# Stores moved from SyncE's DMA queue to ScalarE's in a row softmax with a relative-position bias

## The chip, the core and the metric

The kernel runs on one core of a Trainium2 chip. The metric is the device time of one execution in microseconds (us), the median of several runs. The profile is of one execution of its own.

## What is computed

```python
B, H, S = (2, 8, 2112); max_rel = 16
rel = pos[:, None] - pos[None, :]
bias = rel_bias[:, np.clip(rel, -max_rel, max_rel) + max_rel]
logits = logits + bias[None, :, :, :]
logits = logits - logits.max(axis=-1, keepdims=True)
exp = np.exp(logits)
return exp / exp.sum(axis=-1, keepdims=True)
```

The input `logits` and the output have 2 x 8 x 2112 x 2112 float32 elements, 285.5 MB each. Every element is read once and written once; a row of 2112 elements is one softmax.

## The kernel before

**Tiling.** The 128 partitions hold two heads at a time: 64 partitions for each, and every partition owns 33 consecutive rows of its head (64 x 33 = 2112). An outer loop `k` runs over the 4 pairs of heads. Inside it, 12 chunks `m` (`NT = 12`) run over the 2 batches and over six groups of 6, 5, 6, 5, 6 and 5 of the 33 rows. A chunk is one load and one store of 128 x (6 or 5 rows x 2112) float32, 6336 or 5280 KB; in all there are 48 chunks. Four buffers `X0` to `X3` (`NBUF = 4`) are used in turn, and a chunk is loaded, computed in place and stored from the same buffer.

**Work on a chunk.** VectorE (DVE) adds the bias strip `F` and takes the row's maximum in one instruction for each row (`add`, L173). ScalarE (ACT) does the exp of each row with its sum (`exps`, L181). DVE takes the reciprocals (`scale`, L189) and scales the first three rows (`DV = 3`, L193); ACT scales the other two or three (`scale_rest`, L198). For each pair of heads DVE first builds the strip `F` (`strip`).

**Order.** Every engine has its own hand-written loop, and semaphores tie them: `ld[b]` and `st[b]` count finished loads and stores of buffer b, `added` and `expd` rows, `scaled` and `scaledA` the rows scaled by DVE and ACT. `take(engine, sem, n)` (L82) makes an engine wait for n and take them off again; its waits show as L83.

**DMA queues.** All 48 loads and all stores are issued by SyncE (SP), so they stand in one queue (q1) in program order. ACT's queue (q10) has only the small transfer of the bias table at the start. SP starts with four loads (`load`, L88). Then `turn` does for each n: wait for the scales of chunk n and issue its store (`store`, L96); wait until store n-1 has landed; issue load n+3 into the buffer that has come free. The last chunk's store is issued in two parts, the three rows of DVE and then the others.

Of the kernel before, what the change touches and what calls it, by code (L numbers as in the profile page):

```python
# [11 lines left out]
ENG = mybir.EngineType  # L12
# [3 lines left out]
def kernel(  # L16
# [6 lines left out]
    nc = tc.nc  # L23
    P = 128
    B, H, S, S2 = logits.shape
# [4 lines left out]
    K = H // 2  # L30
# [3 lines left out]
    NBUF = 4  # L34
# [4 lines left out]
    CH = [(b, sum(SIZES[:i]), r) for b in range(B) for i, r in enumerate(SIZES)]  # L39
    NT = len(CH)  # L40
# [3 lines left out]
    X = [io.tile([P, R * S], FP32, tag=f"X{b}", name=f"X{b}") for b in range(NBUF)]  # L44
# [14 lines left out]
    def rows(t, k, m, s0, n):  # L59

        b, j, r = CH[m]
        return bass.AP(
            tensor=t.tensor,
            offset=t.offset + (b * H * S + j + s0) * S + k * (2 * S * S),
            ap=[[W * S, P], [1, n * S]],
        )

    with tc.tile_critical(no_gpsimd_drain=True):  # L68
        ld = [nc.alloc_semaphore(f"ld{b}") for b in range(NBUF)]
        st = [nc.alloc_semaphore(f"st{b}") for b in range(NBUF)]  # L70
        added = nc.alloc_semaphore("added")
        expd = nc.alloc_semaphore("expd")
        scaled = nc.alloc_semaphore("scaled")
        scaledA = nc.alloc_semaphore("scaledA")
# [7 lines left out]
        def take(eng, sem, n):  # L82
            eng.wait_ge(sem, n).then_inc(sem, -n)  # L83


        def load(k, m):
            b, r = m % NBUF, CH[m][2]
            nc.sync.dma_start(out=X[b][:, 0 : r * S], in_=rows(logits, k, m, 0, r)).then_inc(ld[b], 16)  # L88

        def store(k, m, s0=0, n=None):  # L90
            b, n = m % NBUF, n or CH[m][2]
            if s0 < DV:
                take(nc.sync, scaled, DV)
            if s0 + n > DV:
                take(nc.sync, scaledA, s0 + n - DV)
            nc.sync.dma_start(  # L96
                out=rows(out, k, m, s0, n), in_=X[b][:, s0 * S : (s0 + n) * S]
            ).then_inc(st[b], 16)

        for m in range(NBUF):  # L100
            load(0, m)
# [6 lines left out]
            out=bass.AP(tensor=F.tensor, offset=F.offset, ap=[[Q * step, P // Q], [1, H * W]]),  # L108
            in_=bass.AP(tensor=rel_bias.tensor, offset=rel_bias.offset, ap=[[0, P // Q], [1, H * W]]),
# [57 lines left out]
        DV = 3  # L167
# [10 lines left out]
        def exps(m):  # L178
            for i in range(CH[m][2]):
                take(nc.scalar, added, 1)  # L180
                nc.scalar.activation(  # L181
                    out=row(m, i), in_=row(m, i), func=ACTF.Exp, scale=-1.0, bias=col(nmax, m, i),
                    accum_out=col(tot, m, i),
                ).then_inc(expd, 1)

        def scale(m):
            r = CH[m][2]
            take(v, expd, r)
            v.reciprocal(out=col(rec, m, 0, r), in_=col(tot, m, 0, r)).then_inc(inv, 1)  # L189
            v.wait_ge(inv, 1).then_inc(inv, -1)  # L190
            v.sem_inc(invA, 1)
            for i in range(DV):
                v.tensor_scalar_mul(out=row(m, i), in0=row(m, i), scalar1=col(rec, m, i)).then_inc(scaled, 1)  # L193

        def scale_rest(m):
            take(nc.scalar, invA, 1)
            for i in range(DV, CH[m][2]):
                nc.scalar.activation(  # L198
                    out=row(m, i), in_=row(m, i), func=ACTF.Copy, scale=col(rec, m, i),
                ).then_inc(scaledA, 1)  # L200

        with nc.Fori(0, K, 1, engines=[ENG.DVE]) as k:
            strip(k)
            for m in range(NT):
                add(m)
                scale(m)
        with nc.Fori(0, K, 1, engines=[ENG.Activation]):  # L207
            for m in range(NT):
                exps(m)
                scale_rest(m)  # L210

        def turn(k, first, stop):
            for n in range(first, stop):
                store(k + n // NT, n % NT)
                take(nc.sync, st[(n - 1) % NBUF], 16)
                load(k + (n + 3) // NT, (n + 3) % NT)

        store(0, 0)  # L220
        with nc.Fori(0, K - 1, 1, engines=[ENG.SP]) as k:
            turn(k, 1, NT + 1)
        turn(K - 1, 1, NT - 3)
        for m in range(NT - 3, NT - 1):
            store(K - 1, m)
        r = CH[NT - 1][2]
        store(K - 1, NT - 1, 0, DV)
        store(K - 1, NT - 1, DV, r - DV)
        for b in range(NBUF):
            take(nc.sync, st[b], 32 if b == (NT - 1) % NBUF else 16)  # L230


# [28 lines left out]
```

## Time and profile before

| | |
|---|---|
| time, median of 3 runs | 1329.12 us (1329.1 to 1329.44) |
| profiled execution, its time | 1329.3 us |
| its span | 1327.5 us |
| DVE busy / ACT busy | 819.7 us (62%) / 808.8 us (61%) |
| DMA, mean rate over the span | 430 GB/s |
| bytes read from and written to HBM | 285.48 MB and 285.47 MB |

The span is the part of the execution that the profile covers; 1.8 us lie around it. Where a row of the profile names an engine with a q (SPq, ACTq), it is that engine's instruction queue, which issues DMAs and waits on semaphores. A line of DMA issues gives the time from the issue to the landing, including the time in which the transfer stands behind others.

### The profile page before, as it was taken

To read this page: it belongs to the slowest core of one execution; us is meant where nothing else is said; L and a number is where in the kernel's file an instruction comes from. 1 tells how busy PE (TensorE), PEld (TensorE's weight loads), DVE (VectorE), ACT (ScalarE), POOL (GpSimd) and SP (SyncE) were. 2 spreads that over 40 slices of the span, in tenths; PEclk is the share of its full clock that TensorE was granted. 3 is DMA by queue.
4 is the path that set the end of the run, shared out by engine and by line. 5 is a ranking of instruction groups with operands and counts; after the bars stand their busy time and mean duration, and the time that the engine had idled before them with its cause. 6 is when DMAs were issued, how large, how long until landed. Compare 5 with 4: busy or idle time off the path is not lost. (4 is left out here: it accounts for less than half of the span.)

```text
span 1327.5 us, 2383 instructions
## 1 busy us (share of the span) xinstructions
DVE 819.7 (62%) x756; ACT 808.8 (61%) x652; POOL 0.6 (0%) x6
## 2 busy tenths in 40 slices
DVE  6875665558655566556866466664686547665572
ACT  3885575655756557555676566764667646675472
POOL 0000000000000000000000000000000000000000
DMA  9999999999999999999999999999999999999998
GB/s 407 427 424 425 430 433 429 432 431 433 434 430 438 423 439 431 432 432 433 438 436 429 433 430 435 433 430 441 427 439 428 435 431 437 434 436 427 436 427 376
DMA packets 13981, 571.00 MB, mean 430 GB/s; under 512 B 1556, under 2 KB 1560, under 8 KB 1560
## 3 DMA queue, kind: packets, MB, share of 16 engines
q1 hardware_dynamic: 13968, 570.96, 99.8%
q14 instruction: 5, 0.04, 0.0%
q10 hardware_dynamic: 8, 0.00, 0.0%
HBM read 285.48 MB, written 285.47 MB: 430 GB/s over the span
## 5 line engine op out<-in xcount | busy, mean ns | idle before, releaser
L173 DVE CUSTOM_DVE_ANT_0 X<-X,F 128x2112 f32<-128x2112 f32 x264 | 605.5, 2354 | 346.8 <-DVEq L83 346.8
L181 ACT ACTIVATE X<-X,nmax 128x2112 f32<-128x2112 f32 x264 | 542.2, 2054 | 411.5 <-ACTq L83 385.7
L198 ACT ACTIVATE X<-X,rec 128x2112 f32<-128x2112 f32 x120 | 238.7, 2046 | 29.0 <-ACTq L83 29.0
L193 DVE TENSOR_SCALAR X<-X,rec 128x2112 f32<-128x2112 f32 x144 | 181.4, 1316 | 11.6 <-DVEq L190 11.6
L189 DVE RECIPROCAL rec<-tot 128x6 f32<-128x6 f32 (+1 forms) x48 | 9.1, 190 | 116.1 <-DVEq L83 116.1
L181 ACT ACTIVATION_READ_ACCUMULATOR X<-X,nmax 128x1 f32 x264 | 49.3, 187 | 0.0
L181 ACT ACT_TABLE_LOAD x4 | 5.1, 1283 | 55.8 <-ACTq L83 55.8
L173 DVE DVE_READ_ACCUMULATOR2_ANT nmax<- 128x1 f32 x264 | 21.7, 82 | 0.0
L157 DVE TENSOR_TENSOR F<-F,rest 128x2112 f32<-128x2112 f32 x4 | 9.4, 2358 | 0.6
L149 DVE TENSOR_TENSOR F<-Z,rbK 128x2112 f32<-128x2112 f32 x4 | 9.4, 2358 | 0.6
L134 DVE LOAD_MASK_SELECT F<-F x1 | 0.0, 14 | 7.1 <-DMA F<-in_rel_bias_dram 7.1
L155 DVE SCALAR_TENSOR_TENSOR rest<-Z,rbK,rest 128x64 f32<-128x64 f32 x4 | 1.1, 284 | 0.6 <-DVEq L83 0.2
L151 DVE TENSOR_SCALAR rest<-Z,rbK 128x64 f32<-128x64 f32 x4 | 1.1, 275 | 0.0
L105 DVE MEMSET F<- 128x264 f32 x1 | 0.3, 278 | 1.1 <-SPq L68 1.1
L145 DVE COPY rbK<-rbP 128x33 f32 x4 | 0.7, 178 | 0.3 <-DVEq L83 0.3
L153 DVE COPY F<-rbK 128x16 f32<-128x16 f32 x4 | 0.7, 168 | 0.0
L152 DVE COPY F<-rbK 128x16 f32<-128x16 f32 x4 | 0.7, 166 | 0.0
L132 DVE TENSOR_SCALAR Z<-F 128x64 f32<-128x64 f32 x3 | 0.5, 223 | 0.1
L140 DVE COPY rbP<-F 64x132 f32<-64x132 f32 x2 | 0.4, 224 | 0.2
L134 DVE STREAM_SHUFFLE F<-F 128x264 f32<-128x264 f32 x1 | 0.4, 443 | 0.0
L112 POOL IOTA F<- 64x64 f32 x2 | 0.4, 179 | 0.7 <-PEq L256 0.6
L245 POOL MEMSET const-bfloat16-1.0<- 128x1 bf16 x1 | 0.1, 103 | 0.0
(3 smaller groups left out, 0.3 us busy)
## 6 DMA issues: line engine op xcount, KB each, us to landing
X<-in_logits_dram SPq DMA_DIRECT2D x24, 6336.0 KB, 39.7
out_dram<-X SPq DMA_DIRECT2D x24, 6336.0 KB, 46.9
X<-in_logits_dram SPq DMA_DIRECT2D x24, 5280.0 KB, 42.2
out_dram<-X SPq DMA_DIRECT2D x23, 5280.0 KB, 48.6
out_dram<-X SPq DMA_DIRECT2D x1, 3168.0 KB, 16.5
out_dram<-X SPq DMA_DIRECT2D x1, 2112.0 KB, 21.1
F<-in_rel_bias_dram ACTq DMA_DIRECT2D x1, 4.1 KB
```

Source lines behind the costliest of these rows:

```text
L145: then(v.tensor_copy(out=rbK[:, :], in_=rbP[:, bass.ds(k, 1), :]))
L149: then(v.tensor_tensor(out=blocks, in0=view(eq, 0, [[1, NB], [0, W]]), in1=view(rbK, W - 1, [[0, NB], [-1, W]]), op=ALU.mult))
L151: then(v.tensor_scalar(out=rest, in0=lt, scalar1=low, scalar2=None, op0=ALU.mult))
L152: then(v.tensor_copy(out=F[:, 0:MR], in_=low.to_broadcast([P, MR])))
L153: then(v.tensor_copy(out=F[:, FW - MR : FW], in_=high.to_broadcast([P, MR])))
L155: then(v.scalar_tensor_tensor(out=rest, in0=gt, scalar=high, in1=rest, op0=ALU.mult, op1=ALU.add))
L157: then(v.tensor_tensor(out=blocks, in0=blocks, in1=view(rest, 0, [[1, NB], [0, W]]), op=ALU.add))
L173: v.tensor_tensor_reduce(out=row(m, i), in0=row(m, i), in1=F[:, W - 1 - j - i : W - 1 - j - i + S], scale=-1.0, scalar=BIG, op0=ALU.add, o ...
L181: nc.scalar.activation(out=row(m, i), in_=row(m, i), func=ACTF.Exp, scale=-1.0, bias=col(nmax, m, i), accum_out=col(tot, m, i),).then_inc( ...
L189: v.reciprocal(out=col(rec, m, 0, r), in_=col(tot, m, 0, r)).then_inc(inv, 1)
L193: v.tensor_scalar_mul(out=row(m, i), in0=row(m, i), scalar1=col(rec, m, i)).then_inc(scaled, 1)
L198: nc.scalar.activation(out=row(m, i), in_=row(m, i), func=ACTF.Copy, scale=col(rec, m, i),).then_inc(scaledA, 1)
```

## The change

ACT issues each chunk's store itself, directly after its own scales of that chunk: it waits for the three rows of DVE and for its own, and starts the DMA on its own queue. SP keeps the loads alone: it waits until store n has landed and issues load n+4 into the same buffer. The last store is no longer split.

```diff
-        def store(k, m, s0=0, n=None):
-            b, n = m % NBUF, n or CH[m][2]
-            if s0 < DV:
-                take(nc.sync, scaled, DV)
-            if s0 + n > DV:
-                take(nc.sync, scaledA, s0 + n - DV)
-            nc.sync.dma_start(
-                out=rows(out, k, m, s0, n), in_=X[b][:, s0 * S : (s0 + n) * S]
-            ).then_inc(st[b], 16)
+        def store(k, m):
+            b, r = m % NBUF, CH[m][2]
+            take(nc.scalar, scaled, DV)
+            nc.scalar.wait_ge(scaledA, r - DV).then_inc(scaledA, -(r - DV))
+            nc.scalar.dma_start(out=rows(out, k, m, 0, r), in_=X[b][:, 0 : r * S]).then_inc(st[b], 16)
...
-        with nc.Fori(0, K, 1, engines=[ENG.Activation]):
+        with nc.Fori(0, K, 1, engines=[ENG.Activation]) as k:
             for m in range(NT):
                 exps(m)
                 scale_rest(m)
-
-
+                store(k, m)
 
         def turn(k, first, stop):
             for n in range(first, stop):
-                store(k + n // NT, n % NT)
-                take(nc.sync, st[(n - 1) % NBUF], 16)
-                load(k + (n + 3) // NT, (n + 3) % NT)
-
-        store(0, 0)
+                take(nc.sync, st[n % NBUF], 16)
+                load(k + (n + NBUF) // NT, (n + NBUF) % NT)
+
         with nc.Fori(0, K - 1, 1, engines=[ENG.SP]) as k:
-            turn(k, 1, NT + 1)
-        turn(K - 1, 1, NT - 3)
-        for m in range(NT - 3, NT - 1):
-            store(K - 1, m)
-        r = CH[NT - 1][2]
-        store(K - 1, NT - 1, 0, DV)
-        store(K - 1, NT - 1, DV, r - DV)
-        for b in range(NBUF):
-            take(nc.sync, st[b], 32 if b == (NT - 1) % NBUF else 16)
+            turn(k, 0, NT)
+        turn(K - 1, 0, NT - NBUF)
+        for m in range(NT - NBUF, NT):
+            take(nc.sync, st[m % NBUF], 16)
```

## The prediction

> **What bounds the kernel now.** I read the page first: its parts for the engines, the slices, the DMA queues and the DMA issues.
>
> ```profile
> span 1327.5 us, 2383 instructions
> DVE 819.7 (62%) x756; ACT 808.8 (61%) x652; POOL 0.6 (0%) x6
> ...
> DMA  9999999999999999999999999999999999999998
> GB/s 407 427 424 425 430 433 429 432 431 433 434 430 438 423 439 431 432 432 433 438 436 429 433 430 435 433 430 441 427 439 428 435 431 437 434 436 427 436 427 376
> DMA packets 13981, 571.00 MB, mean 430 GB/s; under 512 B 1556, under 2 KB 1560, under 8 KB 1560
> ...
> q1 hardware_dynamic: 13968, 570.96, 99.8%
> ...
> q10 hardware_dynamic: 8, 0.00, 0.0%
> ...
> X<-in_logits_dram SPq DMA_DIRECT2D x24, 6336.0 KB, 39.7
> out_dram<-X SPq DMA_DIRECT2D x24, 6336.0 KB, 46.9
> X<-in_logits_dram SPq DMA_DIRECT2D x24, 5280.0 KB, 42.2
> out_dram<-X SPq DMA_DIRECT2D x23, 5280.0 KB, 48.6
> out_dram<-X SPq DMA_DIRECT2D x1, 3168.0 KB, 16.5
> out_dram<-X SPq DMA_DIRECT2D x1, 2112.0 KB, 21.1
> ```
>
> No compute engine is busy for more than 62%, while packets of queue q1 fill 99.8% of what 16 DMA engines have in the span. The 40 slices are flat; only the first (407) and the last (376) lie well below 430 GB/s. So the kernel lasts as long as its 571 MB take. The windows and the wait lists say whether any stage is different.
>
> ```profile
> 200.00:1200.00 1000.00, 617.61 (x565) 612.19 (x493) 0.00 (x0) 1.00 1.00 433
> 1286.70:1305.30 18.60, 15.41 (x14) 14.74 (x12) 0.00 (x0) 1.00 1.00 433
> 1305.30:1327.50 22.20, 0.00 (x0) 0.00 (x0) 0.00 (x0) 1.00 0.80 346
> 310.90:325.90 15.00, 9.43 (x12) 5.22 (x4) 0.00 (x0) 1.00 1.01 433
> 325.90:340.90 15.00, 13.74 (x12) 12.54 (x12) 0.00 (x0) 1.00 1.00 431
> 340.90:353.70 12.80, 3.99 (x5) 7.04 (x5) 0.00 (x0) 1.00 1.01 429
> 353.70:366.20 12.50, 11.47 (x10) 9.51 (x9) 0.00 (x0) 1.00 1.00 431
> 366.20:381.10 14.90, 3.96 (x4) 5.24 (x4) 0.00 (x0) 1.00 1.01 435
> 381.10:396.10 15.00, 13.76 (x12) 11.84 (x11) 0.00 (x0) 1.00 1.01 436
> ```
>
> ```profile
> ACT X L181 <- ACTq L83: 385.7, 44, 12.5
> ```
>
> ```profile
> SPq L83 <- SPq L83: 1276.6, 141, 36.3
> ```
>
> The last two columns of a window are the DMA share and GB/s. In the middle of the run the DMA share is 1.00 and the rate 433 GB/s. The six short windows are cut where one transfer follows another: the first of each pair is mostly a load, the second mostly a store, and neither direction is slower (433, 429, 435 against 431, 431, 436). The waits say the same from the other side: SP waits 1276.6 of 1327.5 us, and ACT stands 385.7 us in front of its exps because data has not come.
>
> The timeline shows one round of the ring (the engine's waits stand in brackets).
>
> ```profile
> 310.88 0.35 SPq L88 DMA_DIRECT2D X<-in_logits_dram  x1
> ...
> 312.69 3.77 DVE L193 TENSOR_SCALAR X<-X,rec 128x2112 f32<-128x2112 f32 x3 [0.24 <-DVEq L190]
> 312.72 4.00 ACT L198 ACTIVATE X<-X,rec 128x2112 f32<-128x2112 f32 x2 [0.60 <-ACTq L83]
> ...
> 316.87 0.34 SPq L96 DMA_DIRECT2D out_dram<-X  x1
> ...
> 325.88 2.36 DVE L173 CUSTOM_DVE_ANT_0 X<-X,F 128x2112 f32<-128x2112 f32 x1 [3.52 <-DVEq L83]
> ...
> 340.88 0.35 SPq L88 DMA_DIRECT2D X<-in_logits_dram  x1
> ...
> 342.56 3.78 DVE L193 TENSOR_SCALAR X<-X,rec 128x2112 f32<-128x2112 f32 x3 [0.24 <-DVEq L190]
> 342.59 5.95 ACT L198 ACTIVATE X<-X,rec 128x2112 f32<-128x2112 f32 x3 [0.60 <-ACTq L83]
> ...
> 348.68 0.34 SPq L96 DMA_DIRECT2D out_dram<-X  x1
> 353.68 2.36 DVE L173 CUSTOM_DVE_ANT_0 X<-X,F 128x2112 f32<-128x2112 f32 x1 [7.34 <-DVEq L83]
> ...
> 366.19 0.35 SPq L88 DMA_DIRECT2D X<-in_logits_dram  x1
> ...
> 372.31 0.34 SPq L96 DMA_DIRECT2D out_dram<-X  x1
> ```
>
> A transfer of 6336 KB is 6.49 MB, 15.0 us at 433 GB/s, and one of 5280 KB is 12.5 us. Loads are issued at 310.88, 340.88 and 366.19: 30.0 and 25.3 us apart, a load and a store each. The median landing times (39.7 to 48.6 us) are some three transfers: everything stands in one line. A chunk holds its buffer outside that line from the first add to its store: 325.88 to 348.68 is 22.8 us for six rows, 353.68 to 372.31 is 18.6 us for five. Per pair of chunks that is 41.4 of 55.3 us, so on average 0.75 of the four buffers compute and 3.25 wait for or are in a transfer.
>
> **Part 1: two rings in place of one.** The sizes and the number of bytes stay; 48 loads stay on q1, 48 stores go to ACT's queue. Two queues bring no second set of engines: q1 already fills all 16. An engine is idle only when both of its rings are empty, which asks for all four buffers to be in compute at once; with 0.75 there on average that does not occur. So the sum changes only if a packet costs something else when its neighbour is of the other queue and direction. How finely the rings alternate is seen at the start.
>
> ```profile
> 0.97 1.88 SPq L88 DMA_DIRECT2D X<-in_logits_dram  x4
> ...
> 1.39 1.10 ACTq L107 DMA_DIRECT2D F<-in_rel_bias_dram  x1
> ...
> 9.08 0.01 DVE L134 LOAD_MASK_SELECT F<-F  x1 [7.10 <-DMA F<-in_rel_bias_dram]
> ...
> 18.60 2.36 DVE L173 CUSTOM_DVE_ANT_0 X<-X,F 128x2112 f32<-128x2112 f32 x1 [2.15 <-DVEq L83]
> ```
>
> The bias transfer of ACT's queue was issued at about 1.4 us, behind four loads of 23.8 MB, and had landed by 9.08 us, before the first load was used at 18.60. So rings do alternate, and within one transfer. The Trainium skill, page "DMA: Bandwidth & Descriptors", section "Queues, rings and completion order", says that an engine drains a whole packet, typically some 9 to 17 descriptors, from one ring before it goes to the next. By that rule the two rings would alternate about as coarsely as transfers follow each other now, and nothing about directions would change at all. The trace speaks for the finer alternation: a switch every 8 rows would have let the bias through only with the first load. I go by the trace.
>
> The page counts 13981 packets, of which 1556 are under 512 B (16 small ones for each of 97 transfers, and four more). That is 128 large packets to a transfer, 8 on each engine. Today an engine changes direction some 96 times; alternating packet by packet it would do so up to 768 times, 670 more. What a change costs, from both sides:
> - Nothing: the load and store windows above average 432.6 GB/s (weighted by length) and the long window, with the 74 transfers in it, has 433.
> - At most what the reading can hide: one unit in 433 GB/s is 2.3 us in 1000 us, over 74 changes 31 ns, and 670 of those are 21 us.
> - Below nothing: the best window, 436 GB/s, kept through the 1268 us from the first add (18.60) to the last load's landing (1286.7), would save 1268 x 3/436 = 8.7 us.
>
> I take nothing, since that is the row nearest to the case: the rate with changes in it equals the rate between them.
>
> **Part 2: the issue on ACT.** Each chunk puts two waits and one DMA issue behind ACT's scales, and behind these stand the next chunk's exps. An issue costs between 0.34 us (SP's rows) and 1.10 us (ACT's own first one): 48 of them 16 to 53 us on ACT. The 385.7 us of waiting in front of the exps cover that: after the scale that ends at 316.72 the next add comes only at 325.88. The wait for DVE's three scales is short or nil: DVE ends at 316.46 against ACT's 316.72 in five-row chunks, at 346.34 against 348.54 in six-row ones. In the first chunks there is no such cover:
>
> ```profile
> 41.38 16.61 SPq L96 DMA_DIRECT2D out_dram<-X  x2
> 41.48 2.06 ACT L181 ACTIVATE X<-X,nmax 128x2112 f32<-128x2112 f32 x1 [0.20 <-ACTq L83]
> ```
>
> The second chunk's exps would start up to 1.1 us later, and so its store. The four loads need 23.8 MB / 433 GB/s = 55 us, and the first store is there from about 41 us, so the rings are full: nothing on the path.
>
> **Part 3: SP.** SP loses 49 issues; load n+4 waits only for store n, no longer also for the issue of store n+1. That was never the later of the two: the store issued at 316.87 stands before the wait that ends at 340.88. Nothing.
>
> **Part 4: the end.** The last store is no longer split in 3 and 2 rows, so its first part leaves with the second. In the window from 1305.3, where it is issued, 346 GB/s x 22.2 us = 7.7 MB still move, of which the last store is 5.4 MB: 2.3 MB or 5.3 us of older stores stand before it. That covers the lost split, and up to 5.3 us of a later last load. Nothing.
>
> The sum is zero: the profiled execution took 1329.3 us, 1.8 over its span, and the median of the runs is 1329.12. Forecast **1329.0 us**.
>
> **Rivals.**
> *Alternating directions costs* (0.28). For it: no row shows loads and stores alternating packet by packet. Against it: both directions and the mixture run at the same rate. It begins to count at 4 ns for each of the 670 changes (2.7 us) and reaches 21 us at 31 ns. At the middle, 16 ns, it gives 1329 + 11 = 1340 us.
>
> *Alternating helps* (0.13): one ring's end of a transfer lies under the other's packets, and the rate rises to the best window's. 1329 - 8.7 = 1320 us. Against it: a DMA share of 1.00 leaves no gap to fill. The same page of the skill, section "Specifications", gives a ceiling of 435 GB/s; by it the gain would be at most about 6 us, an estimate. The windows at 436 are short enough for that to be rounding.
>
> *The end opens* (0.04): the last load, sharing with a store, lands more than 5.3 us later against the remaining stores, and the engines run dry for the rest. With 12 us later it gives 1329 + 7 = 1336 us.
>
> *The change does not do what it says* (0.03): stores from ACT are served in line with the loads as before, 1329 us. The bias transfer on q10 speaks against it.
>
> **How the numbers follow.** The forecast has 0.52. With the last rival, which gives the same time, "same" (within 0.2%, 2.7 us, about what a measurement here can tell) has 0.55, slower 0.28 + 0.04 = 0.32, faster 0.13. The range runs from 1324 (half of the helping case) to 1345 (16 of the 21 us); outside it lie about 0.07 below and 0.08 above.
>
> **What would show it right or wrong.** Right: q1 and q10 with about 285 MB each, 433 GB/s in the window 200 to 1200 us, loads that land in about 30 us (a 27.5 us pair side by side, plus the completion) in place of 40, stores in 55 to 60 (a buffer's round is four chunks of 27.65 us, less 20.7 of compute and the load's 30). Wrong: a middle window at 430 or less with a DMA share of 1.00 (packets got dearer), at 435 or more (cheaper), a share under 0.99 (both rings empty), or a last window with an earlier fall.

## The result and the profile after

The changed kernel takes 1340.05 us (median of 4 runs, 1337.98 to 1341.81) against 1329.28 us: 1.0079 of the time before, 95% interval 1.0064 to 1.0094. The forecast, no change, failed. The profiled execution took 1341.47 us, one of the slower of the four, with a span 12.1 us longer than before.

From the page of the changed kernel: span, engines, slices, queues, DMA issues (lines left out are marked).

```profile
span 1339.6 us, 2437 instructions
...
DVE 819.6 (61%) x756; ACT 808.4 (60%) x652; POOL 0.6 (0%) x6
...
DMA  9999999999999999999999999999999999999997
GB/s 404 405 422 433 436 432 431 437 431 427 441 430 430 430 436 424 438 430 424 439 432 427 430 428 433 425 431 434 427 427 426 433 427 428 431 425 428 437 433 308
...
q1 hardware_dynamic: 6912, 285.48, 50.0%
q10 hardware_dynamic: 6920, 285.48, 49.3%
...
X<-in_logits_dram SPq DMA_DIRECT2D x24, 6336.0 KB, 37.9
out_dram<-X ACTq DMA_DIRECT2D x24, 6336.0 KB, 49.4
X<-in_logits_dram SPq DMA_DIRECT2D x24, 5280.0 KB, 37.9
out_dram<-X ACTq DMA_DIRECT2D x24, 5280.0 KB, 53.8
```

The engines do the same work, the bytes are split evenly over two queues, and DMA is still the bound. The slices show two losses: many in the second half lie a little lower, and the last one has 308 GB/s where it had 376.

Two windows of the kernel before, then four of the changed one (last two columns: DMA share, GB/s):

```profile
20.00:100.00 80.00, 64.70 (x60) 67.90 (x55) 0.00 (x0) 1.00 1.01 429
1310.00:1320.00 10.00, 0.00 (x0) 0.00 (x0) 0.00 (x0) 1.00 0.94 406
```

```profile
20.00:100.00 80.00, 64.94 (x60) 67.56 (x55) 0.00 (x0) 1.00 1.00 417
200.00:1200.00 1000.00, 618.12 (x566) 610.88 (x494) 0.00 (x0) 1.00 1.00 430
1310.00:1320.00 10.00, 7.35 (x9) 9.00 (x10) 0.00 (x0) 1.00 0.69 299
1320.00:1330.00 10.00, 1.39 (x2) 1.65 (x1) 0.00 (x0) 1.00 0.84 360
```

In the middle the share is 1.00, as before, but the rate is 430 and not 433 GB/s: the engines are never idle, their packets take longer. The queues' part of the DMA view for the window 200 to 1200 us shows whose packets. First the kernel before, then the changed one (packets, MB, share of the 16 engines' time):

```profile
q1 hardware_dynamic: 10471, 433.13, 100.3%
```

```profile
q1 hardware_dynamic: 5200, 214.92, 50.4%
q10 hardware_dynamic: 5220, 215.33, 49.8%
```

Share divided by MB gives the price of a byte: per cent of the 16 engines' time in 1000 us for each MB. Before it is 100.3 / 433.13 = 0.2316. Afterwards stores (q10) pay 49.8 / 215.33 = 0.2313 and loads (q1) 50.4 / 214.92 = 0.2345, 1.3% more than before. Over 215 MB that is 0.63% of 1000 us, 6 us. The packet records show that not every load pays: in this window 9.4% of the load packets took over 50 ns more than the usual 1.56 us (five rows, 42,240 bytes) or 1.87 us (six rows), against 0.5% of the store packets, and 1.2% of all packets before. Half of these long load packets are among the first two behind the end of a store on their engine.

The accounts of this one execution: in the middle window the DMA view gives 430.27 MB moved against 433.16, 2.9 MB or 6.7 us behind. What it loses from 20 to 100 us (417 against 429 GB/s) is made up between 100 and 200 and after 1200 us. So some 6.7 us are lost by 1290 us, and the other 5.4 of the 12.1 us after that, where the share falls to 0.69. The first row below is the last chunk's first add in the kernel before; the others are the changed kernel's timeline:

```profile
1286.66 2.36 DVE L173 CUSTOM_DVE_ANT_0 X<-X,F 128x2112 f32<-128x2112 f32 x1 [7.08 <-DVEq L83]
```

```profile
1264.62 0.33 SPq L88 DMA_DIRECT2D X<-in_logits_dram  x1
...
1298.98 0.34 ACTq L94 DMA_DIRECT2D out_dram<-X  x1
...
1303.29 2.36 DVE L169 CUSTOM_DVE_ANT_0 X<-X,F 128x2112 f32<-128x2112 f32 x1 [6.73 <-DVEq L83]
...
1321.87 0.34 ACTq L94 DMA_DIRECT2D out_dram<-X  x1
```

The last load's chunk begins at 1303.29 instead of 1286.66, and its store is issued at 1321.87. The DMA view of the end gives that store 16.6 us, and the store before it, issued at 1298.98, 27.0 us for 15 us of data: it landed at 1326.0, after the last one was issued. So part of the DMA engines idled while others were still busy. For each transfer the trace has sixteen 4-byte completion packets, one of each engine. From first to last they lie 4.1 us apart at the end of the kernel before. In the changed kernel they lie some 16 us apart for most stores, and 5 to 7 us for loads.

### The profile page after: what moved, and what is told of

Read it like the earlier page. It is cut to its first block, busy times and chain, and to the rows that moved or that the text cites. A ratio compares the mean times of both kernels' runs of the same rounds, so it can differ in the third digit from the quotient of the medians.

```text
span 1339.6 us, 2437 instructions
## 1 busy us (share of the span) xinstructions
DVE 819.6 (61%) x756; ACT 808.4 (60%) x652; POOL 0.6 (0%) x6
## 5 line engine op out<-in xcount | busy, mean ns | idle before, releaser
L189 DVE TENSOR_SCALAR X<-X,rec 128x2112 f32<-128x2112 f32 x144 | 181.3, 1315 | 11.6 <-DVEq L186 11.6
## 6 DMA issues: line engine op xcount, KB each, us to landing
X<-in_logits_dram SPq DMA_DIRECT2D x24, 6336.0 KB, 37.9
out_dram<-X ACTq DMA_DIRECT2D x24, 6336.0 KB, 49.4
X<-in_logits_dram SPq DMA_DIRECT2D x24, 5280.0 KB, 37.9
out_dram<-X ACTq DMA_DIRECT2D x24, 5280.0 KB, 53.8
```

## The experiments

**Is it ACT?** Everything on ACT's queue, in the order of the kernel before (the code cuts below are shortened; `...` marks what is left out):

```diff
-            nc.sync.dma_start(out=X[b][:, 0 : r * S], ...)
+            nc.scalar.dma_start(out=X[b][:, 0 : r * S], ...)
...
                 exps(m)
+                take(nc.scalar, st[(m + 2) % NBUF], 16)
+                load(k + (m + 2) // NT, (m + 2) % NT)
                 scale_rest(m)
                 store(k, m)
```

> All loads and stores are issued by ACT on its one queue, in the order of the kernel before (the load of chunk m+2 between ACT's exps and scales of chunk m); SP issues nothing. Theory 'directions' (loads and stores alternating packet by packet make packets dearer) and theory 'end' (the last load lands late because it shares the engines with stores): one ring, so no alternation, 1329 us within 2, middle window 200 to 1200 us at 433 GB/s. Theory 'ACT' (the issue or the waits on ACT's instruction stream cost the time): as slow as the changed kernel or slower, 1338 us or more.

It took 1368.54 us, for a reason that neither theory had. Its windows:

```profile
20.00:100.00 80.00, 35.55 (x37) 29.73 (x25) 0.00 (x0) 1.00 0.60 260
...
200.00:1200.00 1000.00, 619.76 (x568) 610.08 (x493) 0.00 (x0) 1.00 1.00 432
```

The small bias transfer, on ACT's queue too, stood behind four loads in one ring and was used at 58.61 us instead of 9.08, which held the start back; the middle is at 432 GB/s. With that transfer alone on SP:

> As the run with everything on ACT's queue, but the bias table is loaded by SP: before, it stood behind the four first loads in ACT's own ring, which held all computation back for some 40 us at the start. Theory 'directions' and 'end': 1329 us within 2, middle window at 432 to 433 GB/s. Theory 'ACT': 1338 us or more still.

1332.95 us, 1.0025 (1.0014 to 1.0036), the middle at 433 GB/s: ACT's issues and waits cost the middle nothing. The 3.4 us that stay come after 1290 us, where completion packets lie 9.7 us apart: the last chunk's first add starts at 1291.21 us, 4.6 us later than before, though by 1290 us as many bytes have moved. Why the packets spread there was not tried.

**Is it the end?** First the changed kernel with its last four stores handed to SP, in the old order; then the old order with only the last four stores on ACT's queue.

```diff
-        turn(K - 1, 0, NT - NBUF)
+        turn(K - 1, 0, NT - NBUF - 1)
+        store_sp(K - 1, NT - 4)
+        turn(K - 1, NT - NBUF - 1, NT - NBUF)
+        for m in range(NT - 3, NT):
+            store_sp(K - 1, m)
```

> The changed kernel, but the last four stores go to SP's queue in the order of the kernel before (store 44, load 47, stores 45, 46, 47); ACT only releases them. Theory 'end': the gap in the DMA share before the last store closes, about 5 us less than the changed kernel, 1333 to 1336 us; the middle window stays at 430 GB/s by theory 'directions'. If the end costs nothing, it stays at 1338 to 1342 us.

1339.62 us: nothing came back. The last load is still issued at 1264.36 us (1264.62 in the changed kernel, 1244.01 before), and its first add starts at 1297.14. The window still shows the hole:

```profile
1310.00:1320.00 10.00, 3.97 (x4) 4.90 (x4) 0.00 (x0) 1.00 0.74 320
```

> The counterpart: the kernel before, with stores 0 to 43 on SP in its order, and only the last four stores on ACT's queue. Theory 'end': 3 to 6 us more than the kernel before, 1332 to 1335 us, with a gap in the DMA share before the last store and the middle window at 433 GB/s. If the whole difference is dearer packets: 1329 to 1330 us.

1344.65 us, 1.0109 (1.0092 to 1.0125), with the middle at 433 GB/s: 14.6 us, where 3 to 6 were expected. Its last load lands late and the engines run dry:

```profile
1261.98 0.34 SPq L88 DMA_DIRECT2D X<-in_logits_dram  x1
```

```profile
1290.00:1300.00 10.00, 10.00 (x9) 7.38 (x7) 0.00 (x0) 1.00 0.74 321
1300.00:1310.00 10.00, 7.35 (x8) 9.14 (x8) 0.00 (x0) 1.00 0.01 4
```

So two rings at the end can open a hole, but handing over the last four stores alone does not close the changed kernel's. With the last 12 chunks in one ring:

> Two queues for stores 0 to 35 as in the changed kernel, then one queue (SP) in the order of the kernel before for the last 12 chunks, so that the engines have 300 us in one ring before the end. Theory 'end': the gap before the last store closes (DMA share over 0.9 up to 1320 us) and about 5 us come back; of the dearer packets three quarters stay: 1333 to 1336 us. If the end plays no part: 1337 to 1338 us.

1334.71 us (1334.12 to 1337.32), in the range of theory "end", but without its sign:

```profile
200.00:1200.00 1000.00, 622.51 (x571) 616.34 (x499) 0.00 (x0) 1.00 1.00 432
...
1310.00:1320.00 10.00, 2.81 (x3) 3.06 (x2) 0.00 (x0) 1.00 0.77 331
```

The hole stays (0.77), since 300 us in one ring leave the spread as it is: 11.6 us up to the last chunks. The gain came from the middle, and in part by chance: up to about 1020 us this run and the changed kernel have the same two queues, yet from 200 to 1000 us it moved 345.6 MB against 344.6 (346.3 before). The run with the last four stores on SP shows the same: with the changed kernel's order of transfers it moved 432.01 MB between 200 and 1200 us, 2.7 us behind instead of 6.7:

```profile
q1 hardware_dynamic: 5225, 216.19, 50.3%
q10 hardware_dynamic: 5230, 215.79, 49.9%
```

So how dear the same middle is differs between executions. A reading of the end: dearer packets fall unevenly on the engines, the spread stays, and the engine that is last sets when the last load has landed and when the kernel ends. That reading joins these two runs, the 9.7 us with everything on ACT's queue, and the spreads; no run tests it alone.

**Is it the directions?** The transfers without computation: loads on SP into two buffers, stores on ACT out of two others (constants), in two queues, in one, and on two queues that always move the same way.

```diff
+        def stream(eng, b0, sems, into):
+            for n in range(M):
+                if n >= 2:
+                    take(eng, sems[n % 2], 16)
+                move(eng, n, b0 + n % 2, sems[n % 2], into)
...
+        stream(nc.sync, 0, ld, True)
+        stream(nc.scalar, 2, st, False)
```

> No computation: 48 loads on SP's queue into two buffers, beside 48 stores on ACT's queue out of two others, with no dependence between them. Leaves out all of the softmax; only the transfers are left. Theory 'directions': middle window at 429 to 430 GB/s, and loads take over 1% more engine time for their bytes than stores. If dearer packets come from the order of the kernel (short rings, waits) or from DVE and ACT at work in SBUF: 433 GB/s and the same time per byte in both queues.

> The same transfers without computation, loads and stores in turn on SP's queue alone, two of each in flight. All theories: 433 GB/s in the middle.

> The same transfers without computation on two queues, but never loads beside stores: first all 48 loads, the even ones on SP's queue and the odd ones on ACT's, then all stores, split in the same way. Theory 'directions': 433 GB/s in the middle of each half, since both rings move the same way. If it is the switch from ring to ring that costs: 430 GB/s in both halves.

One queue has 433 GB/s in the middle (1356.2 us, some 28 of them waiting for memsets). Two queues in the same direction have 432 (1328.86 us): going from ring to ring costs nothing. Loads beside stores cost far more than expected, 1531.82 us. The middle window of that run, its queues there, and two of its issues:

```profile
200.00:1200.00 1000.00, 0.00 (x0) 0.00 (x0) 1.00 1.00 376
```

```profile
q10 hardware_dynamic: 4554, 188.19, 52.3%
q1 hardware_dynamic: 4554, 188.22, 47.4%
```

```profile
389.66 28.88 SPq L91 DMA_DIRECT2D X<-in_logits_dram  x2
389.86 28.89 ACTq L93 DMA_DIRECT2D out_dram<-X  x2
```

At a full share loads pay 0.252 and stores 0.278 a MB instead of 0.2316. So directions matter, but 13% of the rate is not the 0.7% of the changed kernel, and the pattern is another one: here stores pay most (81% of their packets took over 50 ns longer than usual, 25% of the loads'), there only loads pay. Three runs move the stores to other places of the output (`(n + M - d) % M` for n):

> The transfers alone on two queues, but store n writes the place of chunk n-4 (as in the real kernel, where a load runs three or four chunks ahead of the store beside it), not that of the load beside it. If the 376 GB/s of the first such run came from loads and stores at the same offsets of the two tensors: back to 428 to 433 GB/s in the middle. If it comes from loads and stores that run free beside each other (no common pace between the engines): 376 GB/s again.

> The same with store n at the place of chunk n-24, two head pairs away. Offsets matter: 428 to 433 GB/s. Free running: 376 GB/s. If only the distance in memory counts, this one and the one at 4 chunks differ.

> The free-running transfers on two queues again, with store n at the place of chunk n-3, so that a transfer of six rows always runs beside one of five, as in the changed kernel. If the equal lengths of the pair (in step packet by packet) make the 376 GB/s: over 420 GB/s. If not: 376 GB/s.

376, 377 and 375 GB/s in the middle (1529.99, 1529.52 and 1528.07 us): neither the distance in memory nor the equal lengths do it. Next the real buffers and dependences without computation, `take(eng, ld[n % NBUF], 16)` ahead of each store and `take(eng, st[n % NBUF], 16)` ahead of each load:

> The changed kernel's transfers with its real dependences and buffers but without computation: loads on SP, stores on ACT, store n after load n has landed, load n+4 after store n (it leaves out the whole softmax and copies the logits). If the free-running transfers are slow (376 GB/s) because nothing ties loads and stores together: 428 to 432 GB/s in the middle, 1330 to 1345 us. If any loads beside stores are that slow once no computation separates them: 376 GB/s, 1500 us.

1422.35 us, neither of the two: it begins at full rate and loses it later. Its windows, and its issues at an early and a late time:

```profile
100.00:600.00 500.00, 0.00 (x0) 1.00 1.00 431
700.00:1200.00 500.00, 0.00 (x0) 1.00 0.97 391
```

```profile
404.99 0.34 ACTq L93 DMA_DIRECT2D out_dram<-X  x1
411.18 0.33 SPq L91 DMA_DIRECT2D X<-in_logits_dram  x1
```

```profile
916.59 0.34 ACTq L93 DMA_DIRECT2D out_dram<-X  x1
916.78 0.33 SPq L91 DMA_DIRECT2D X<-in_logits_dram  x1
```

While store and load are issued 6.2 us apart, the rate is almost the usual one; when they have drifted to 0.2 us, as in the free run, stores pay 0.256 and loads 0.239 (700 to 1200 us). The share of 0.97 says that a smaller part of the loss is idle time. The other reading was that the engines lose step, so two runs keep them in step: pairs that start together with a barrier between, and one transfer in flight in each queue.

```diff
-                if n >= 2:
-                    take(eng, sems[n % 2], 16)
+                if n:
+                    take(eng, sem, 16)
+                    eng.sem_inc(mine, 1)      # the run in pairs only
+                    take(eng, other, 1)       # the run in pairs only
```

> The free-running transfers on two queues, but in pairs: load n on SP and store n on ACT start together, and neither queue goes on before both have landed, so that the sixteen engines begin every pair in step. It loses time between pairs; what counts is the engine time per byte in each queue (share of the 16 engines divided by MB, 0.2316 per cent of 1000 us in the kernel before). If the engines' loss of step makes packets dear: near 0.2316 in both queues. If loads beside stores are dear as such: near the 0.252 (loads) and 0.278 (stores) of the first free-running run.

> The free-running transfers on two queues, with one transfer in flight in each instead of two, and no tie between the queues. The rings run short for a moment after each transfer, which also brings the engines of a ring back into step at each transfer. If packets are dear because both rings always hold the next transfer, or because the engines lose step: near 0.2316 per cent per MB. If loads beside stores are dear as such: 0.252 and 0.278 as before.

Each was run once, so only their prices are read here. Queues in the window 200 to 1200 us, first of the pairs, then of one in flight:

```profile
q1 hardware_dynamic: 4128, 170.18, 46.5%
q10 hardware_dynamic: 4128, 170.04, 44.1%
```

```profile
q10 hardware_dynamic: 5256, 217.76, 50.3%
q1 hardware_dynamic: 5205, 214.35, 49.9%
```

The pairs pay 0.273 and 0.259, though the engines of a transfer finish within some 2 us of each other: step is no cure. One in flight pays 0.233 and 0.231, little more than usual. It has only about half as many changes of direction, though: followed along each engine (in the records a packet starts within 4 ns of the end of the one before it), 45% of the large packets come behind one of the other queue, against 99% in the first free run; where one queue has just ended a transfer, several packets of the other follow each other. And the transfers of the two queues settle apart: measured by the middle of the completion packets, loads end by turns 0.33 and 0.43 of the way through a store's round. So the offset alone was changed next, in the free run, by holding the first store back with a memset:

```diff
+        nc.vector.wait_ge(zero, 2)
+        nc.vector.memset(X[3][:, 0:8700], 1.0).then_inc(zero, 1)
...
-        nc.scalar.wait_ge(zero, 2)
+        nc.scalar.wait_ge(zero, 3)
```

> The free-running transfers on two queues, two in flight in each, changed in nothing but the start of the stores: one more memset of 7.3 us on DVE holds the first store back by about half a load. In the runs so far packets were dear where load and store were issued within 0.2 us of each other round after round, and at the usual price where they stood half a transfer apart. Theory 'phase': the offset persists, since the rings alternate packet by packet, and the middle window is at 428 to 433 GB/s. If free running or two in flight make packets dear: 376 GB/s as before.

> The same with the stores held back by 15 us, a whole load, so that load and store start together again. Theory 'phase': 375 to 390 GB/s. If it was the later start as such: as fast as with half a transfer.

Half a transfer off took 1340.76 us, against 1531.82 with the same transfers. Its middle window, and two loads and one store:

```profile
200.00:1200.00 1000.00, 0.00 (x0) 0.00 (x0) 1.00 1.00 432
```

```profile
387.12 26.82 SPq L91 DMA_DIRECT2D X<-in_logits_dram  x2
...
404.28 0.34 ACTq L93 DMA_DIRECT2D out_dram<-X  x1
```

The store stands 17.2 us behind the load, and by the completion packets the offset stays at 0.35 to 0.40 of a round up to the last loads. Changes of direction are as many as in the first free run in the same window (8,107 against 7,998), so it is not their number that costs. The second delay missed its aim, since the first store's packets began some 4 us after its issue: the offset became 0.61 to 0.65, not 0 or 1, and the rate 433 GB/s (1334.04 us). So it is a second offset without a price, not the counter-test that it was meant to be. That test is the first free run, whose offset is 1.00 throughout.

For the changed kernel the same measure gives 0.60 to 0.65 in its first 500 us and then a drift to some 0.80; its rate goes from 432 GB/s (200 to 700 us) to 429 (700 to 1200 us). In the run with the last four stores on SP, which has the same middle, the offset goes from about 0.5 to about 0.4 at 1050 us, and the rates are 433 and 431. So neither comes near 0 or 1.00, where the transfers alone were dear, and only loads pay there, unlike in the runs in step. The kept traces also show a price that grows at a steady offset: in the run half a transfer off, long load packets (over 50 ns above the usual) went from 3.9% (100 to 350 us) to 8.6% (900 to 1200 us), and in the changed kernel from 1.1% (100 to 200 us) to 5.1% (350 to 500 us), while the completion packets spread further (stores: from 1 to 16 us in the one, from 10 to 13 us in the other). What sets the changed kernel's price is therefore open, and the spread is a rival to the offset that no run separates. Open as well is what makes packets dear when loads and stores start together; and no run put the changed kernel's order of waits into one queue.

## Why the prediction failed, step by step

**Part 1, the failed step.** "I take nothing, since that is the row nearest to the case." The rows behind it had transfers that follow each other in one ring; none had a load beside a store. Measured: loads pay 1.3% more and the middle loses 6.7 us, and in another execution of the same order of transfers 2.7 us. Keeping 16 of the 21 us in the range was right. The rival "alternating directions costs" came out at its time, 1340 us, which is in part luck: it gave all 11 us to the changes of direction, while 5.4 of 12.1 us lie at the end. Its price for each change is not the mechanism either: half a transfer off makes as many changes at 432 GB/s as the start in step makes at 376. In the transfers alone the offset of the two rings decides, which the prediction did not consider; what sets the price in the changed kernel, whose offset is never that of the dear run, stays open.

**The argument on idle engines held** in the middle: the DMA share stays at 1.00. The rule of coarse alternation that Part 1 cites from the Trainium skill would have changed nothing about directions; the runs decide against it. In the run in pairs the load and the store of six rows both land 38.7 to 38.8 us after they were issued together, where turns of a whole transfer would set them some 15 us apart. The Trainium skill, page "DMA: Bandwidth & Descriptors", section "Issuing engines are not separate DMA queues", says that transfers started by different engines run on the same DMA engines, interleave, and save only issue time. The trace agrees that nothing is gained; that something is lost, 376 against 433 GB/s at worst, the rule does not say.

**Part 2 held.** ACT's wait ahead of its exps is longer than before, not shorter:

```profile
ACT X L177 <- ACTq L83: 400.2, 48, 19.8
```

With everything on ACT the middle ran at 433 GB/s.

**Part 3 held** in that no lack of issues shows. **Part 4 failed**, the second step. It put the end at nothing and allowed the last load 5.3 us; its chunk began 16.6 us later, of which some 6.7 are what the middle had lost. "The end opens" had 0.04 at 1336 us; an end loss of 5.4 us came on top of the middle's. Its mechanism would give 16.6 - 6.7 - 5.3 = 4.6 us here, so the size fits. It is not the whole, because the hole stayed with the old order at the end, where the last load was later by less (8.0 us with the last 12 chunks in one ring). The spread of the engines goes with the hole; that it makes it is argued, not shown.

**Landing times.** Loads were to land in about 30 us and took 37.9; stores in 55 to 60 and took 49.4 and 53.8. The load's ring holds more than the one load that was assumed.

## What to carry to other kernels

Where one queue already fills the DMA engines, a second one has nothing to give, and loads beside stores cost between nothing and 13% of the rate here. With transfers alone that depended on how far apart the two queues stand, which one queue in a fixed order settles. And in a kernel bound by DMA, look at the engine that is last, not only at the mean share: here the runs with everything on ACT's queue and with the end in one queue, whose engines finished a transfer 9.7 to 13 us apart, lost some 4 to 6 us of the span after 1290 us.

## What was not expected of the hardware

- Loads and stores on two queues run at 376 GB/s when they start within 0.2 us of each other round after round, and at 432 to 433 when 0.33 to 0.65 of a round apart; two queues in the same direction run at 432.
- The offset is kept for a thousand us by free-running queues, and drifts under dependences: the copy went from 431 to 391 GB/s by itself, in part with idle engines (share 0.97).
- A transfer of 4.1 KB behind four loads on one queue was used at 58.61 us, and the start ran at 260 GB/s from 20 to 100 us; on the other queue it was used at 9.08 us.
- The same transfers in two queues fell 2.7 us behind in one execution and 6.7 us in another, in the same 1000 us.
